# Row normalisation on one core: sharing the last scale between two engines, storing the last tile from ScalarE's queue, and issuing only the first load ahead of the entry barrier

## The chip, the core and the metric

The kernel runs on one core of a Trainium2 chip. The core has several engines that run their own instruction streams and meet through semaphores. Four matter here: VectorE (DVE in the profile), ScalarE (ACT), GpSimd (POOL) and SyncE (SP). TensorE (PE) has no work. Data moves between the device memory (HBM, here called DRAM in the names) and the on-chip memory of 128 partitions by 16 DMA engines, which take transfers from queues. A transfer is issued by an instruction of one engine, and that engine's name is the queue's name in this text.

The metric is the time of one execution on the device in microseconds (us). The median of three runs is 81.77 us, the lowest 81.73 and the highest 81.94.

## The reference

```python
def setup_inputs():
    batch, dim = 1024, 4096
    return {"x": np.random.randn(batch, dim).astype(np.float32), "axis": -1, "eps": np.float32(1e-12)}

def reference(x, axis, eps):
    norm = np.sqrt(np.sum(x ** 2, axis=axis, keepdims=True) + eps)
    return (x / norm).astype(np.float32)
```

Each of 1024 rows of 4096 float32 is divided by the root of its sum of squares. 16.78 MB are read and 16.78 MB written.

## The kernel before, in words

The 1024 rows are cut into two tiles (called tile 0 and tile 1 below). A tile has 128 partitions with R = 4 rows of 4096 values in each, 64 KB in a partition and 8.39 MB in all. Both tiles have their own buffer `xt`, so nothing waits for a buffer to come free. A tile is loaded by one transfer (line 219), scaled in place, and stored by one transfer (line 239). All four transfers are issued by SP.

For each tile (lines 223 to 239) the four rows of a partition are taken as follows. DVE squares and sums row 3 (`square_dve`, line 42) and ACT squares and sums rows 0, 1 and 2 one after the other (`square_act`, line 33). `norm` takes the root on ACT (line 53) and the reciprocal on DVE (line 59). `scale` multiplies a row by its reciprocal norm on DVE (line 64). The rows are scaled in the order 0, 1, 3, 2. For row 2, the last one, tile 0 uses `scale_by_both`: ACT takes the first 7/8 of the columns (3584, line 72) and DVE the remaining 512 (line 78). Tile 1 uses the plain `scale` on DVE. The store of a tile waits for all of its scales.

The program begins with an entry barrier: each engine arrives, GpSimd gathers the arrivals and releases all. `to_front` moves a load out of the body and in front of SP's arrival (its `Drain`) in the entry block. Before the change it is called for both loads, in the order of the tiles, so that SP issues both and then arrives.

At the end there are two barriers (line 271 in the profile). `gpsimd_waits_for_last_store` rewrites the second one: SP waits for everything except the last store before it arrives, and GpSimd, which gathers, waits for the last store's landing before it releases the others. Its argument is the store of tile 1; it finds that store by its semaphore, on whichever queue it is issued.

Of the kernel before, what the change touches and what calls it, by code (L numbers as in the profile page):

```python
# [79 lines left out]
        )  # L80


def to_front(nc, load):

    def move(program):  # L90
        blocks = program.main_func.blocks
        entry = blocks[0].instructions
        if any(i.name == load.name for i in entry):
            return
        body = next(
            b.instructions
            for b in blocks
            if any(i.name == load.name for i in b.instructions)
        )
        at = next(n for n, i in enumerate(body) if i.name == load.name)  # L100
        assert not body[at].sync_info.on_wait
        before = next(
            n
            for n, i in enumerate(entry)
            if i.engine == mybir.EngineType.SP and isinstance(i, mybir.InstDrain)
        )
        entry.insert(before, body.pop(at))

    nc.at_finalize(move)
# [72 lines left out]
@with_exitstack  # L182
def kernel(
    ctx: ExitStack,
    tc: tile.TileContext,
    x: bass.AP,
    axis: bass.AP,
    eps: bass.AP,
    out: bass.AP,
):  # L190
    nc = tc.nc
    P = nc.NUM_PARTITIONS

    assert isinstance(axis, int) and axis in (-1, len(x.shape) - 1)
    eps = float(eps)

    x = x.flatten_outer_dims()
    out_flat = out.flatten_outer_dims()
    N, D = x.shape
    R = 4  # L200
    assert N % (P * R) == 0
    n_tiles = N // (P * R)
    x_t = x.rearrange("(p t r) d -> t p (r d)", t=n_tiles, r=R)
    out_t = out_flat.rearrange("(p t r) d -> t p (r d)", t=n_tiles, r=R)

    io = ctx.enter_context(tc.tile_pool(name="io", bufs=n_tiles))
    scratch_pool = ctx.enter_context(tc.tile_pool(name="scratch", bufs=1))
    stats = ctx.enter_context(tc.tile_pool(name="stats", bufs=n_tiles))

    eps_t = scratch_pool.tile([P, 1], F32)  # L210
    nc.vector.memset(eps_t, eps)  # L211
    sq_act = scratch_pool.tile([P, D], F32)
    sq_dve = scratch_pool.tile([P, D], F32)
    scratch = {"act": sq_act, "dve": sq_dve}

    groups = []
    for i in range(n_tiles):
        g = RowGroups(nc, io, stats, scratch, D, R, eps_t)
        load = nc.sync.dma_start(out=g.flat(), in_=x_t[i])  # L219
        to_front(nc, load.ins)  # L220
        groups.append(g)

    for i, g in enumerate(groups):
        g.square_dve(R - 1)
        g.square_act(0)
        g.norm(0)
        g.scale(0)
        g.square_act(1)
        g.norm(1)
        g.norm(R - 1)  # L230
        g.scale(1)
        g.scale(R - 1)
        g.square_act(2)
        g.norm(2)
        if i < n_tiles - 1:
            g.scale_by_both(2)
        else:
            g.scale(2)
        store = nc.sync.dma_start(out=out_t[i], in_=g.flat())
    gpsimd_waits_for_last_store(nc, store.ins)  # L240


# [33 lines left out]
```

## Time and profile before

The profiled execution took 81.77 us. Its span, from the first to the last instruction of the kernel, is 79.9 us; the remaining 1.87 us lie around the span.

| What | Value |
|---|---|
| Time of the profiled execution | 81.77 us |
| Span | 79.9 us |
| DVE busy | 26.7 us (33%) |
| ACT busy | 29.7 us (37%) |
| DMA queue busy, share of 16 engines | 97.6% |
| Bytes moved, mean rate over the span | 33.55 MB, 420 GB/s |
| Squares on ACT (line 33), each | 3609 ns |
| Square on DVE (line 42), each | 4424 ns |
| Scale of a row on DVE (line 64), each | 2353 ns |
| ACT's part of the shared scale (line 72) | 3282 ns |
| DVE's part of the shared scale (line 78) | 486 ns |

All times in the views count from the span's start. In a line of the timeline the first number is the start, the second the duration, then follow the engine, the line of the kernel, the operation and its operands; a bracket at the end tells the idle time before it and what ended it. A letter q behind an engine's name (SPq) means its sequencer, which issues transfers and waits. In the DMA view a row of numbers divides the window in equal slices; a packet's bytes are counted in the slice in which it begins. "To landing" is the time from a transfer's issue to its last completion.

### The profile page before, as it was taken

The numbers are of one execution on the slowest core, as the hardware profiler recorded it, in microseconds if no ns is written. First come the engines' busy times: TensorE is split into PE (matmuls) and PEld (weight loads), VectorE is DVE, ScalarE is ACT, GpSimd is POOL, SyncE is SP. The second block draws the span as 40 slices with busy tenths as digits, with TensorE's granted clock in tenths as the row PEclk, the third lists the DMA queues.
The fourth block names the chain that finished last, engine by engine and source line by source line (L and its number), as shares of the span: only waits on it lengthen the run. The fifth ranks groups of instructions, "written<-read, shape, count | busy, mean of one in ns | idle before, by whom it ended". The sixth has DMA issues, their size and how long they took to land.

```text
span 79.9 us, 93 instructions
## 1 busy us (share of the span) xinstructions
DVE 26.7 (33%) x21; ACT 29.7 (37%) x23; POOL 0.2 (0%) x4
## 2 busy tenths in 40 slices
DVE  0000000000099599960049995999200000000000
ACT  3200000000099999989349999950000000000000
POOL 1000000000000000000000000000000000000000
DMA  9099996599996699993899991999974999965990
GB/s 492 33 525 525 525 525 295 230 525 525 525 525 262 262 525 525 525 525 164 361 525 525 525 459 66 525 525 525 525 328 197 525 525 525 525 295 230 525 525 0
DMA packets 576, 33.55 MB, mean 420 GB/s; under 512 B 64, under 2 KB 64, under 8 KB 64
## 3 DMA queue, kind: packets, MB, share of 16 engines
q1 hardware_dynamic: 576, 33.55, 97.6%
HBM read 16.78 MB, written 16.78 MB: 420 GB/s over the span
## 4 chain that ended last, share of the span: by engine, by line
DMA 51%; ACT 10%; DVE 9%; SPq 0%; issue 0%
DMA xt<-in_x_dram 51%; ACT sq_act L33 9%; DVE xt L64 9%; ACT rstd L53 1%; SPq L219 0%; DVE rstd L59 0%
## 5 line engine op out<-in xcount | busy, mean ns | idle before, releaser
L33 ACT ACTIVATE sq_act<-xt 128x4096 f32<-128x4096 f32 x6 | 21.7, 3609 | 21.7 <-DMA xt<-in_x_dram 21.7
L42 DVE SCALAR_TENSOR_TENSOR sq_dve<-xt 128x4096 f32<-128x4096 f32 x2 | 8.8, 4424 | 25.7 <-DMA xt<-in_x_dram 25.7
L64 DVE TENSOR_SCALAR xt<-xt,rstd 128x4096 f32<-128x4096 f32 x7 | 16.5, 2353 | 0.2
L72 ACT ACTIVATE xt<-xt,rstd 128x3584 f32<-128x3584 f32 x1 | 3.3, 3282 | 0.2 <-DVE rstd L59 0.2
L53 ACT ACTIVATE rstd<-ssq,eps_t 128x1 f32<-128x1 f32 x8 | 2.1, 289 | 0.1
L59 DVE RECIPROCAL rstd<-rstd 128x1 f32<-128x1 f32 x8 | 1.3, 159 | 2.4 <-ACT rstd L53 2.4
L33 ACT ACT_TABLE_LOAD x1 | 1.3, 1283 | 1.3 <-PEq L257 1.3
L53 ACT ACT_TABLE_LOAD x1 | 1.3, 1283 | 0.0
L33 ACT ACTIVATION_READ_ACCUMULATOR sq_act<-xt 128x1 f32 x6 | 1.1, 186 | 0.0
L211 DVE MEMSET eps_t<- 128x1 f32 x1 | 0.1, 59 | 1.3 <-PEq L257 1.3
L78 DVE TENSOR_SCALAR xt<-xt,rstd 128x512 f32<-128x512 f32 x1 | 0.5, 486 | 0.0
L42 DVE DVE_READ_ACCUMULATOR sq_dve<-xt 128x1 f32 x2 | 0.2, 82 | 0.0
L257 POOL MEMSET const-bfloat16-1.0<- 128x1 bf16 x1 | 0.1, 103 | 0.0
L257 POOL MEMSET const-uint8-127<- 128x1 uint8 x1 | 0.1, 102 | 0.0
L257 POOL MEMSET const-float32-0.0<- 128x1 f32 x1 | 0.1, 100 | 0.2 <-issue 0.2
L257 POOL MEMSET const-float32-1.0<- 128x1 f32 x1 | 0.1, 99 | 0.0
## 6 DMA issues: line engine op xcount, KB each, us to landing
xt<-in_x_dram SPq DMA_DIRECT2D x2, 31.2
out_dram<-xt SPq DMA_DIRECT2D x2, 22.5
```

Source lines behind the costliest of these rows:

```text
L33: self.nc.scalar.activation(out=sq_a, in_=self.x[:, r], func=ACT_F.Square, accum_out=self.ssq[:, r : r + 1],)
L42: self.nc.vector.scalar_tensor_tensor(out=sq_v, in0=self.x[:, r], scalar=1.0, in1=self.x[:, r], op0=ALU.mult, op1=ALU.mult, accum_out=self ...
L53: self.nc.scalar.activation(out=self.rstd[:, r : r + n], in_=self.ssq[:, r : r + n], func=ACT_F.Sqrt, bias=self.eps_t,)
L59: self.nc.vector.reciprocal(out=self.rstd[:, r : r + n], in_=self.rstd[:, r : r + n])
L64: self.nc.vector.tensor_scalar_mul(out=self.x[:, r], in0=self.x[:, r], scalar1=self.rstd[:, r : r + 1])
L72: self.nc.scalar.activation(out=self.x[:, r, :cut], in_=self.x[:, r, :cut], func=ACT_F.Copy, scale=rstd,)
L78: self.nc.vector.tensor_scalar_mul(out=self.x[:, r, cut:], in0=self.x[:, r, cut:], scalar1=rstd)
L211: nc.vector.memset(eps_t, eps)
L257: nc = _bacc.Bacc("TRN2", target_bir_lowering=False, num_devices=1)
```

## The change

Three things change. Only the first tile's load is moved ahead of SP's arrival at the entry barrier; the second tile's load stays in the body and is issued behind the barrier, still by SP. (The function that moves it gets a new name; its body is the same.) The last row of tile 1 is scaled as that of tile 0 is, by ACT and DVE together. And the store of tile 1 is issued by ACT, on ACT's queue, while that of tile 0 stays with SP.

```diff
-def to_front(nc, load):
+def first_load_to_front(nc, load):
...
         load = nc.sync.dma_start(out=g.flat(), in_=x_t[i])
-        to_front(nc, load.ins)
+        if i == 0:
+            first_load_to_front(nc, load.ins)
         groups.append(g)
...
         g.square_act(2)
         g.norm(2)
-        if i < n_tiles - 1:
-            g.scale_by_both(2)
-        else:
-            g.scale(2)
-        store = nc.sync.dma_start(out=out_t[i], in_=g.flat())
+        g.scale_by_both(2)
+        queue = nc.sync if i < n_tiles - 1 else nc.scalar
+        store = queue.dma_start(out=out_t[i], in_=g.flat())
     gpsimd_waits_for_last_store(nc, store.ins)
```

## The prediction, made before the changed kernel was run

> **What bounds the kernel now.** I read the head of the page and its DMA rows first, to see which resource is full.
>
> ```profile
> span 79.9 us, 93 instructions
> DVE 26.7 (33%) x21; ACT 29.7 (37%) x23; POOL 0.2 (0%) x4
> q1 hardware_dynamic: 576, 33.55, 97.6%
> ```
>
> The reader is to see that both computing engines are idle for nearly two thirds of the span while the one DMA queue is busy for 97.6% of it. 576 packets are 512 of data and 64 small ones (the page counts 64 under 512 B), so a data packet is 33.55 MB / 512 = 65.5 KB, and each of the 16 engines moves 32 of them.
>
> Next the four transfers, by their issues and the median time to landing (load 0 alone takes 21.8 us to land and load 1 40.7, since the minimum and maximum for the tile are 21.8 and 40.7; the stores take 21.8 and 23.3).
>
> ```profile
> xt<-in_x_dram SPq DMA_DIRECT2D x2, 31.2
> out_dram<-xt SPq DMA_DIRECT2D x2, 22.5
> 0.00 0.86 SPq L219 DMA_DIRECT2D xt<-in_x_dram  x2
> 38.71 0.35 SPq L239 DMA_DIRECT2D out_dram<-xt  x1
> 56.50 0.34 SPq L239 DMA_DIRECT2D out_dram<-xt  x1
> ```
>
> Landings follow: load 0 at 0.0 + 21.8 = 21.8, load 1 at 0.43 + 40.7 = 41.1, store 0 at 38.7 + 21.8 = 60.5, store 1 at 56.5 + 23.3 = 79.8. The distances are 19.3, 19.4 and 19.3 us, that is, every transfer lands one full transfer time after the one ahead of it, whatever the moment of its issue. The whole span is therefore 21.8 (cold start and first load) + 19.3 + 19.4 + 19.3 = 79.8, and 0.1 for the release at the end. Nothing on the ACT or DVE side is a term of that sum as long as each transfer is queued before the one ahead runs dry.
>
> How early must it be queued? The DMA view over five-microsecond windows answers, since it books a packet where it begins (rates of 1500 to 3100 GB/s in slices of 0.125 us are whole packets counted at once). In order: 0 to 5, 38 to 43 and 58 to 63 us.
>
> ```profile
> GB/s 0 0 0 0 0 0 0 0 3146 2621 0 0 1049 0 524 524 524 0 0 0 0 0 0 0 0 0 0 0 0 0 0 0 1573 3146 524 2097 1049 0 0 0
> ...
> GB/s 1049 1573 2097 0 0 0 0 0 0 0 0 0 0 0 0 0 0 0 2097 2097 1049 2097 1049 0 0 0 0 0 0 0 0 0 0 0 0 0 0 1573 2097 1049
> ...
> GB/s 0 0 0 0 0 0 0 0 0 0 0 0 0 3146 1573 1573 2097 0 0 0 0 0 0 0 0 0 0 0 0 0 0 0 2097 2621 1573 1573 524 0 0 0
> ```
>
> First row: after a cold issue at 0.0 the first packets begin at 1.0 to 2.1 us, and the second round at 4.0 to 4.6. A round in steady state is 19.3 / 8 = 2.4 us, so the cold lag is worth 1.6 to 2.2 us from issue to a packet at full pace. Second row: store 0, issued at 38.71, has its first packets at 40.25 to 40.9, one round after those at 38.0 to 38.4: 1.5 us of lead is enough on this queue, with no hole. Third row: the round that begins at 59.6 to 60.1 is store 1's first. This is the appointment that the changed kernel has to keep.
>
> Last the end of each tile on the engines, and what SP still waits for.
>
> ```profile
> 35.41 3.28 ACT L72 ACTIVATE xt<-xt,rstd 128x3584 f32<-128x3584 f32 x1 [0.23 <-DVE rstd L59]
> 35.41 0.49 DVE L78 TENSOR_SCALAR xt<-xt,rstd 128x512 f32<-128x512 f32 x1
> 53.93 0.15 DVE L59 RECIPROCAL rstd<-rstd 128x1 f32<-128x1 f32 x1
> 54.12 2.35 DVE L64 TENSOR_SCALAR xt<-xt,rstd 128x4096 f32<-128x4096 f32 x1
> SPq L271 <- PEq L271: 19.4, 2, 19.2
> SPq L271 <- DMA out_dram<-xt: 3.2, 1, 3.2
> ```
>
> Store 1 is issued at 56.5, as soon as the 2.35 us scale ends, 3.1 us ahead of 59.6. SP then waits 3.2 us for store 0 and 19.2 us at the exit barrier while store 1 drains.
>
> **The change, part by part.** *First load.* It stays ahead of the barrier at 0.0. Same packets, same 1.0 us: 0.
>
> *Second load.* Its issue (0.43 us) leaves the place ahead of SP's arrival. SP arrives some 0.43 us sooner, at about 0.5 in place of 0.9. GpSimd, the gatherer, has ended its four memsets (the last begins at 0.33 and takes 0.10) and its own drain (0.18 from 0.30) by then, so the barrier falls at about 0.8 in place of 1.2. ACT's first table load and DVE's memset start 0.4 us sooner and then wait for load 0 until 21.8 as before: worth 0. The load itself goes out at about 0.8 and is through by 1.3, some 0.4 later than before. Its first packets are due at 21.0 (1.0 + 8 rounds of 2.4 + the lag), so 19 us of load 0 cover it, and nothing stands between the barrier and it on SP. If that cover were gone it would cost 0.4.
>
> *The shared last scale.* One 2.35 us DVE scale becomes an ACT copy of 3584 columns (3.28 us in tile 0) beside a DVE scale of 512 (0.49). ACT is free: its last work in tile 1 ends at 53.1. The reciprocal that both need still stands behind DVE's scale of row R-1, ends at 54.08, and the next instruction starts at 54.12. ACT then runs 54.12 to 57.40, DVE ends at 54.6. So the sharing makes the last row ready 3.28 - 2.35 = 0.93 us later, not sooner.
>
> *The store on ACT's queue.* ACT issues it behind its own copy, about 57.42 (SP took 0.02 us after the copy in tile 0: 35.41 + 3.28 = 38.69, issue at 38.71). Nothing else of the kernel is queued behind it on ACT but its exit arrival, which moves from about 53 to about 57.8; DVE's arrival (after 54.6) and SP's (after store 0's issue) are sooner. The first of the two exit barriers then closes near 58 in place of 57, and the second one waits for store 0 at 60.5 and then store 1 at 79.8 in any case: 0.
>
> The lead over 59.6 is 59.6 - 57.42 = 2.2 us, against 3.1 before. The trace shows no DMA issued by ACT, so its lag is bounded by two rows: 1.5 us on a running queue (no loss, 0.7 to spare) and 1.6 to 2.2 us on a cold one (57.42 + 2.2 = 59.6: just in time). A loss is open above: if nothing of the cold lag overlaps store 0, it is paid from the landing at 60.5 to 62.7, against 60.1 before, +2.6 us. A gain is excluded here, since the engines have no idle time between 41 and 79 to win back. I take 0, by the cold row, which is the nearest: ACT's queue is as unused at 57.4 as SP's is at 0.0, and the engines are busy with store 0 while it starts.
>
> *Two queues at once.* Store 0's last round starts at 57.2 to 57.7 (59.6 to 60.1 less 2.4), and a cold queue brings its first packets 1.0 us after 57.42, at 58.4. So store 0 has no unstarted packets to interleave with: 0.
>
> The sum: 21.8 + 19.3 + 19.4 + 19.3 + 0.1 = 79.9 us again, and the 1.87 us around the span (81.77 - 79.9). The profiled execution took 81.77, which is also the median shown, so no shift is needed: 81.8 us.
>
> The page "DMA: Bandwidth & Descriptors" of the Trainium skill gives, under "Latency and other measured facts", about 0.6 us to the first byte of a DMA issued from SP or ACT. The first row above has 1.0 to 2.1 us, so the measurement stands; by the page the store would reach the engines at 58.0, with 1.6 us to spare, and the sum would be the same 81.8. The same page, under "Issuing engines are not separate DMA queues", says that DMAs from different engines share the 16 DMA engines and that spreading them saves the issue time alone. That speaks against a gain from ACT's queue: what it could save is SP's 0.34 us issue, which here lies under store 0, so by the rule as by the sum nothing is won.
>
> **The rivals.** (A, slower) ACT's queue starts late. It decides from a lag of 2.2 + 0.25 us after 57.42. For it: the lead shrinks from 3.1 to 2.2, exactly the slow end of the cold lag, and the start of a second queue beside a running one is in no row. Against it: at 38.71 a lead of 1.5 was enough. Price: half as long again as the cold lag, 3.3 us, puts the first packets at 60.7 against 59.6 to 60.1, +0.6 to +1.1, so +0.9: 82.7 us. The whole lag behind store 0's landing would give 84.4.
>
> (B, faster) The second load's issue disturbs the first one's start. The first packets spread over 1.0 to 2.1 us, while the second load's issue ran at 0.43 to 0.86, just ahead of them. If its absence let all engines start a second issue's length sooner, 0.43 us would be won at the front of a gapless chain: 81.35. Against it: the second issue only moves to 0.8 to 1.3, right into the first packets, and eleven of sixteen first packets begin within the first quarter of a microsecond. Moved there it may even disturb more.
>
> (C, slower) A second queue costs something at the launch or the end, in the 1.87 us around the span, which no row breaks up. By one more issue's length, 0.35: 82.1.
>
> (D) The change does not do what it says: ACT's part is not the last to end, or the barrier is held by something else. Either leaves the DMA chain as it is: 81.8, inside the forecast.
>
> **How the numbers follow.** Forecast with D 0.54, A 0.24, C 0.08, B 0.14. Within 0.3% (0.25 us, about what a measurement of this kernel can tell from no change; its three runs span 81.73 to 81.94) is the forecast alone: 0.54. Slower is A and C, 0.32; faster is B, 0.14. The likeliest case alone has 81.6 to 82.0. The range has to reach B's price and A's middle price: 81.4 to 82.7; what is left out is the dearer half of A and the tail of B, under 2 in 10.
>
> **What would show it.** Right: the first load's packets from 1.0 us, the second load's issue at 0.8 to 0.9, landings again near 21.8, 41.1, 60.5 and 79.8, an ACT issue at 57.4, and the DMA view over 58 to 63 with a full round at 59.6 to 60.1 and the next one 2.4 us later. Rival A is a hole in that view, with store 1's landing later by the same amount and SP's exit wait longer. Rival B is a first round closer together and every landing earlier by the same few tenths, from 21.8 on. Rival C leaves the span at 79.9 and lengthens the time alone. The prediction is wrong above all if ACT's first DMA needs more than 2.4 us to bring a packet to an engine.

## The result and the profile after

The changed kernel takes 82.72 us (median of 6 runs, 82.59 to 82.83) where the kernel before took 81.88 (81.73 to 81.98): the ratio is 1.0103, with a 95% interval of 1.0087 to 1.0119. It is slower by 0.84 us. The forecast was no change, and the upper end of its range, 82.7, is 0.02 us short of the median.

The profiled execution took 82.78 us. The first lines of its page, its span and its two DMA queues (packets, megabytes, share of 16 engines), are these:

```profile
span 80.9 us, 94 instructions
...
q1 hardware_dynamic: 432, 25.17, 72.9%
q10 hardware_dynamic: 144, 8.39, 24.9%
```

A second queue, q10, now carries one of the four transfers. The span grew by 1.0 us and the time around it stayed at 1.9 (82.78 - 80.9), so the loss is inside the kernel. The page's list of issues, with the median time to landing, places it:

```profile
xt<-in_x_dram SPq DMA_DIRECT2D x2, 31.2
out_dram<-xt SPq DMA_DIRECT2D x1, 21.8
out_dram<-xt ACTq DMA_DIRECT2D x1, 23.2
```

The timeline has the end of tile 1 on ACT:

```profile
54.28 3.28 ACT L72 ACTIVATE xt<-xt,rstd 128x3584 f32<-128x3584 f32 x1 [1.04 <-DVE rstd L59]
57.59 0.37 ACTq L238 DMA_DIRECT2D out_dram<-xt  x1
```

ACT issues store 1 at 57.59 and it lands 23.2 us later, at 80.8. Store 0 (issued at 38.82) lands at 60.6. Between the two lie 20.1 us, where the kernel before had 19.3. That is 0.8 of the 1.0 us; the other 0.2 is a slightly later landing of both loads in this execution (21.9 and 41.3 in place of 21.8 and 41.1). That part comes and goes: of two runs below with the same two loads, the profiled execution of the one with 2048 columns on ACT has 21.9 and 41.3 too, and that of the one with 4064 has 21.7 and 41.1.

The DMA view, which books a packet where it begins, shows what happened within that transfer. The rows are the windows from 57 to 62 and from 60 to 65 us, in slices of 0.125 us:

```profile
GB/s 0 0 0 2621 2097 2621 524 524 0 0 0 0 0 0 0 0 0 0 0 0 0 0 1049 2622 3670 0 1049 0 0 0 0 0 0 0 0 0 0 0 0 0
...
GB/s 3670 0 1049 0 0 0 0 0 0 0 0 0 0 0 0 0 0 0 0 0 0 0 0 0 0 3670 3670 1049 0 0 0 0 0 0 0 0 0 0 0 0
```

Store 0's last round begins at 57.4 to 57.9, and store 1's first round at 59.8 to 60.4, one packet time of 2.4 us later. So far there is no hole. But store 1's second round does not begin until 63.1 to 63.5. In the view of before, from 58 to 63 us, the round of 59.6 to 60.1 was followed by one at 62.0. The packet records say the same: the sixteen first packets of store 1 last 3.07 to 3.48 us, while every other packet of both stores lasts 2.42. All sixteen engines lose 0.65 to 1.06 us once, in the packet with which they go over from SP's queue to ACT's.

A first packet of that length has one other place in this profile. The first packets of load 0, which start cold, last 2.86 to 3.37 us here. By these rows the hand-over to the other queue costs about what a cold start costs beyond its issue (0.44 to 0.95 us more than 2.42); that the two have one cause is not shown.

### The profile page after: what moved, and what is told of

Read it like the earlier page. It is cut to its first block, busy times and chain, and to the rows that moved or that the text cites. A ratio compares the mean times of both kernels' runs of the same rounds, so it can differ in the third digit from the quotient of the medians.

```text
span 80.9 us, 94 instructions
## 1 busy us (share of the span) xinstructions
DVE 24.9 (31%) x21; ACT 33.0 (41%) x24; POOL 0.2 (0%) x4
## 4 chain that ended last, share of the span: by engine, by line
DMA 50%; ACT 14%; DVE 6%; issue 0%
DMA xt<-in_x_dram 50%; ACT sq_act L33 9%; DVE xt L64 6%; ACT xt L72 4%; ACT rstd L53 1%; DVE rstd L59 0%
## 5 line engine op out<-in xcount | busy, mean ns | idle before, releaser
L33 ACT ACTIVATE sq_act<-xt 128x4096 f32<-128x4096 f32 x6 | 21.7, 3608 | 22.4 <-DMA xt<-in_x_dram 22.4
L64 DVE TENSOR_SCALAR xt<-xt,rstd 128x4096 f32<-128x4096 f32 x6 | 14.1, 2353 | 0.2
L72 ACT ACTIVATE xt<-xt,rstd 128x3584 f32<-128x3584 f32 x2 | 6.6, 3283 | 1.3 <-DVE rstd L59 1.3
L78 DVE TENSOR_SCALAR xt<-xt,rstd 128x512 f32<-128x512 f32 x2 | 1.0, 486 | 0.1
## 6 DMA issues: line engine op xcount, KB each, us to landing
out_dram<-xt SPq DMA_DIRECT2D x1, 21.8
out_dram<-xt ACTq DMA_DIRECT2D x1, 23.2
```

Of the source, the lines that this page charges most:

```text
L33: self.nc.scalar.activation(out=sq_a, in_=self.x[:, r], func=ACT_F.Square, accum_out=self.ssq[:, r : r + 1],)
L64: self.nc.vector.tensor_scalar_mul(out=self.x[:, r], in0=self.x[:, r], scalar1=self.rstd[:, r : r + 1])
L72: self.nc.scalar.activation(out=self.x[:, r, :cut], in_=self.x[:, r, :cut], func=ACT_F.Copy, scale=rstd,)
L78: self.nc.vector.tensor_scalar_mul(out=self.x[:, r, cut:], in0=self.x[:, r, cut:], scalar1=rstd)
```

## The experiments

Ratios are to the kernel before, run on the same chip beside each group of kernels (medians 81.80 to 81.84 us).

**Which part.** Four kernels do the parts one by one. The first is the kernel before with only the store moved to ACT.

```diff
-        store = nc.sync.dma_start(out=out_t[i], in_=g.flat())
+        queue = nc.sync if i < n_tiles - 1 else nc.scalar
+        store = queue.dma_start(out=out_t[i], in_=g.flat())
```

> The kernel before with one part of the change: store 1 is issued by ACT (both loads ahead of the barrier, last scale on DVE alone). The issue should be near 56.5, a lead of about 3.1 us over store 0's end instead of 2.2. New-queue theory (the first packet of each DMA engine on a queue that takes over takes 3.1 to 3.5 us in place of 2.4, whatever the lead): the same 0.65 to 1.05 us longer first round, time +0.7 to +0.9 us, ratio 1.009 to 1.011. Lateness theory (the store was issued too late): with 0.9 us more lead most or all of it goes, time within 0.1 us of before, first round at 2.4 us.

Measured: 81.81 us, ratio 1.0003 (0.9988 to 1.0017). The second is the kernel before with only the last scale shared.

```diff
-        if i < n_tiles - 1:
-            g.scale_by_both(2)
-        else:
-            g.scale(2)
+        g.scale_by_both(2)
```

> The kernel before with one part of the change: the last scale of tile 1 is shared by ACT and DVE, store 1 is issued by SP near 57.4. New-queue theory: no second queue, so nothing: within 0.1 us of before, packets at 2.4 us throughout. Lateness theory: the lead of 2.2 us is as short as in the changed kernel, so the same loss of 0.7 to 0.9 us.

Measured: 81.79 us, ratio 0.9986 (0.9978 to 0.9995). The third moves only the second load.

```diff
-        to_front(nc, load.ins)
+        if i == 0:
+            to_front(nc, load.ins)
```

> The kernel before with one part of the change: only the first load is ahead of the barrier. Both theories put nothing here, within 0.1 us. Third theory (the move of the second load disturbs the start or the loads): +0.1 to +0.2 us, as the changed kernel's load landings of 21.9 and 41.3 stand 0.1 and 0.15 behind those of before.

Measured: 81.81 us, ratio 1.0000 (0.9991 to 1.0009). The fourth is the changed kernel with its last store back on SP.

```diff
-        queue = nc.sync if i < n_tiles - 1 else nc.scalar
-        store = queue.dma_start(out=out_t[i], in_=g.flat())
+        store = nc.sync.dma_start(out=out_t[i], in_=g.flat())
```

> The changed kernel with store 1 given back to SP (shared last scale and the second load behind the barrier stay). New-queue theory: within 0.1 us of before. Lateness theory: still +0.7 to +0.9 us. Third theory: +0.1 to +0.2 us.

Measured: 81.83 us, ratio 1.0000 (0.9990 to 1.0010).

No part loses anything by itself. The second load's place is worth nothing, which disposes of the third theory. A store from SP that is issued as late as in the changed kernel (57.52 in the fourth) loses nothing, so the short lead alone is not the cause. A store from ACT that is issued at 56.47 loses nothing either, so the other queue alone is not the cause, and the new-queue theory falls in the form "whatever the lead". (The second kernel's interval ends just below 1; its 0.14% is less than the 0.3% called no change.) The loss needs both: ACT's queue, and the 0.93 us by which the shared scale delays the issue. In the first run the view from 60 to 65 us has its second round at 62, at full pace:

```profile
GB/s 524 0 0 0 0 0 0 0 0 0 0 0 0 0 0 1049 2621 1573 2097 524 524 0 0 0 0 0 0 0 0 0 0 0 0 0 0 2621 1573 3146 524 524
```

**Lag or boundary.** Two theories can hold for that combination. In one, ACT's issue needs a fixed 3.2 to 3.4 us to reach full pace, and what the lead lacks is lost. In the other, an engine that has already begun the last packet of the old queue when the new queue's work arrives pays a fixed price. The next two kernels move the issue to both sides by changing ACT's share of tile 1's last row; tile 0 keeps its 7/8.

```diff
-    def scale_by_both(self, r):
-        cut = 7 * self.D // 8
+    def scale_by_both(self, r, cut):
...
-        g.scale_by_both(2)
+        g.scale_by_both(2, 7 * D // 8 if i < n_tiles - 1 else 2816)
```

> The changed kernel, with ACT's part of tile 1's last scale cut from 3584 to 2816 columns (DVE takes 1280). ACT's part should take about 0.30 + 0.00083 x 2816 = 2.64 us instead of 3.28, so store 1 is issued by ACT near 56.9 in place of 57.6, a lead of about 2.9 us. Fixed-lag theory (a store issued by ACT beside SP's running queue needs about 3.2 to 3.4 us from issue to full pace: 57.59 to the first round's ends 63.2 to 63.4 less one packet time of 2.42): full pace at 60.2 in place of 59.6 to 60.1, time +0.2 to +0.4 us against before. Boundary theory (an engine that finds the other queue's packet only after it has begun its last one pays a fixed 0.65 to 1.05 us, else nothing): each first packet at 2.4 or at 3.1 to 3.5 us, nothing between, time 0 or +0.85.

Measured: 82.42 us, ratio 1.0074 (1.0058 to 1.0090), that is +0.62; issue at 56.91. As times go, both theories missed here: the lag had +0.2 to +0.4, the boundary 0 or +0.85. The packets decide.

```diff
-        g.scale_by_both(2)
+        g.scale_by_both(2, 7 * D // 8 if i < n_tiles - 1 else 4064)
```

> The changed kernel, with ACT's part of tile 1's last scale raised from 3584 to 4064 columns (DVE takes 32). ACT's part about 3.68 us, issue near 58.0, a lead of about 1.8 us. Fixed-lag theory: full pace at 61.3, first packets of about 3.5 to 3.9 us or a hole of that size, time +1.2 to +1.3 us against before. Boundary theory: the same 3.1 to 3.5 us as in the changed kernel, time +0.85.

Measured: 82.62 us, ratio 1.0096 (1.0079 to 1.0113), that is +0.82; issue at 57.76.

The fixed lag asked for +1.2 to +1.3 in the second of these and got +0.82, the same as the changed kernel: it falls. The first, with 2816 columns, shows the boundary itself. Its rows from 57 to 62 and from 60 to 65 us:

```profile
GB/s 0 1049 2097 2621 1573 524 524 0 0 0 0 0 0 0 0 0 0 0 0 0 0 2097 3146 2097 524 524 0 0 0 0 0 0 0 0 0 0 0 0 0 0
...
GB/s 524 524 0 0 0 0 0 0 0 0 0 0 0 0 0 0 0 0 1049 524 1049 0 0 2097 2097 1573 0 0 0 0 0 0 0 0 0 0 0 1049 524 524
```

In the second row a slice of 524 is one packet. Five engines begin their second packet at 62.2 to 62.6, and eleven at 62.9 to 63.25; in the packet records the five first packets last 2.42 to 2.44 us and the eleven 3.10 to 3.43, with nothing between. The records do not name the engine, but a packet begins 2 ns behind the end of the one ahead of it, so each first packet can be paired with a last one. The engines that had begun store 0's last packet up to 0.49 us behind the issue (56.91) are all long, those that began it 0.64 us or more behind are all at full pace, and between 0.5 and 0.64 there are both. So the boundary runs through the middle of the round here, eleven engines pay and five do not, and the time lies between the two that the theory had allowed. The same rule sorts the other runs: in the changed kernel all last packets begin between 0.16 us before and 0.30 us behind the issue (all sixteen long), in the run with only the store moved between 0.67 and 1.20 us behind it (none long).

The Trainium skill's page "DMA: Bandwidth & Descriptors" ("Latency and other measured facts") gives about 0.6 us from the issue on SP or ACT to the first byte. The boundary at 0.5 to 0.64 us is of that size; that it is the same thing, the time until an engine can know of the new queue's work, is not shown. The shortest time from an issue to a packet on idle engines in these runs is 0.86 us (58.71 to 59.57, in the run with the queues exchanged below). The prediction had put the page's figure aside for the 1.0 us that the first load needs at the start.

**Shift the boundary from the other side.** If the rule holds, the change can be kept whole, queue and sharing included, and cost nothing, provided ACT's share is small enough.

```diff
-        g.scale_by_both(2)
+        g.scale_by_both(2, 7 * D // 8 if i < n_tiles - 1 else 2048)
```

> The changed kernel with ACT's part of tile 1's last scale cut from 3584 to 2048 columns (DVE takes 2048). ACT's part about 2.0 us, store 1 issued by ACT near 56.3, over 0.65 us ahead of the start of store 0's last packets (57.1 to 57.9). Boundary theory: no long first round, time within 0.15 us of before (ratio 0.998 to 1.002).

Measured: 81.78 us, ratio 0.9992 (0.9982 to 1.0002); issue at 56.30, and the second round stands at 61.9 to 62.7 in the window from 60 to 65 us:

```profile
GB/s 524 524 0 0 0 0 0 0 0 0 0 0 0 0 0 1049 2097 524 2097 2097 0 524 0 0 0 0 0 0 0 0 0 0 0 0 0 2621 524 2621 1573 524
```

It is as fast as the kernel before, not faster: no version here beats the DMA chain.

**First use of a queue.** In the next kernel ACT issues a small load into an unused tile at the start, beside the changed kernel's work, so that its queue is no longer new at 57 us.

```diff
+    warm = scratch_pool.tile([P, 16], F32)
+    first = nc.scalar.dma_start(out=warm, in_=x_t[0][:, :16])
+    first_load_to_front(nc, first.ins)
...
+    engine = load.engine
...
-            if i.engine == mybir.EngineType.SP and isinstance(i, mybir.InstDrain)
+            if i.engine == engine and isinstance(i, mybir.InstDrain)
```

> The changed kernel with one more transfer: at the start, ahead of its arrival, ACT issues a load of 128 partitions x 16 columns (8 KB) into an unused tile, so that store 1 is not the first transfer on ACT's queue. If the lag is that of a queue's first use: it is gone, time within 0.2 us of before. If it belongs to each start of a queue that had run empty, or to ACT: still +0.7 to +0.9 us.

Measured: 82.82 us, ratio 1.0124 (1.0103 to 1.0145). All sixteen first packets of store 1 last 3.08 to 3.48 us. The loss does not belong to a queue's first use.

**Does it belong to ACT?** A first attempt to exchange the queues missed its aim.

```diff
-        load = nc.sync.dma_start(out=g.flat(), in_=x_t[i])
+        load = nc.scalar.dma_start(out=g.flat(), in_=x_t[i])
...
-            if i.engine == mybir.EngineType.SP and isinstance(i, mybir.InstDrain)
+            if i.engine == mybir.EngineType.Activation and isinstance(i, mybir.InstDrain)
...
-        queue = nc.sync if i < n_tiles - 1 else nc.scalar
+        queue = nc.scalar if i < n_tiles - 1 else nc.sync
```

> The changed kernel with the two queues exchanged: ACT issues both loads (the first ahead of its own arrival) and store 0, SP issues store 1 near 57.5. If the lag belongs to ACT's issues: SP needs no more than the 1.5 to 2.2 us that the trace of before shows, so the first round of store 1 runs at 2.4 us and the time is within 0.15 us of before. If it belongs to any queue that starts beside a running one: first round again 3.1 to 3.5 us, +0.7 to +0.9 us.

Measured: 100.98 us, ratio 1.2351 (1.2326 to 1.2377). With the loads on ACT the scheduler put DVE's square of tile 1 ahead of tile 0's scales, so store 0 went out at 58.7 and the DMA engines stood empty from about 41 to 59 us. It says nothing on the hand-over it was made for. It shows two other things. Store 0 restarted engines that had stood empty for over 18 us, on ACT's queue, which had moved the loads, and its sixteen first packets lasted 2.44 to 2.46 us. So a queue that has run empty, or an engine that has stood idle, does not make a first packet long by itself. And store 1, issued by SP at 70.6 while store 0 was under way, ran beside it. In the window from 74 to 79 us, with the packets of each queue below,

```profile
GB/s 0 6816 1573 0 0 0 0 0 0 0 0 0 0 0 0 0 0 0 0 0 4194 4194 0 0 0 0 0 0 0 0 0 0 0 0 0 0 0 0 0 2621
...
q10 hardware_dynamic: 21, 1.38, 63.6%
q1 hardware_dynamic: 16, 1.05, 48.4%
```

the round at 74.1 is ACT's, that at 76.6 is SP's and that at 78.9 ACT's again, each 2.42 us behind the last. Going from queue to queue is free here, while both have work waiting. The same page of the Trainium skill, under "Queues, rings and completion order", has each engine take turns between its queues packet by packet; these three rounds agree. The order ahead of them is not explained: SP had issued at 70.6, and the rounds of 71.7 and 74.1 were both still ACT's.

The aimed test keeps the loads on SP. Store 0 goes out from ACT, store 1 from ACT or from SP, and one more ACT copy of 1024 columns into scratch delays store 1 until store 0's last packets have begun.

```diff
-    def scale_by_both(self, r):
+    def scale_by_both(self, r, rest):
...
+        if rest:
+            self.nc.scalar.activation(
+                out=self.scratch["act"][:, :rest],
+                in_=self.x[:, r, :rest],
+                func=ACT_F.Copy,
+                scale=rstd,
+            )
...
-        g.scale_by_both(2)
-        queue = nc.sync if i < n_tiles - 1 else nc.scalar
+        g.scale_by_both(2, rest=0 if i < n_tiles - 1 else 1024)
+        queue = nc.scalar
```

> The changed kernel with both stores on ACT's queue, and with one ACT copy of 1024 columns into scratch (1.05 us) ahead of tile 1's last scale, so that store 1 is issued near 58.7, behind the start of store 0's last packets (58.1 to 58.7). Boundary theory (only a hand-over to another queue pays, and pays once): store 0 is issued near 38.8, behind the start of load 1's last packets, so its first round runs 3.1 to 3.5 us; store 1's first round, on the same queue, runs 2.42 us; time +0.8 to +0.9 us against before. If every late issue by ACT pays: both rounds long, +1.6 to +1.8 us.

Measured: 82.57 us, ratio 1.0088 (1.0075 to 1.0102), that is +0.74. The last line of the edit becomes, in its companion, one with SP for store 1:

```diff
-        queue = nc.scalar
+        queue = nc.scalar if i < n_tiles - 1 else nc.sync
```

> As the run with both stores on ACT's queue (store 0 from ACT, the same ACT copy of 1024 columns into scratch), but store 1 is issued by SP, near 58.7. Boundary theory: the hand-over from SP to ACT at store 0 pays, and that from ACT back to SP at store 1 pays too, first rounds 3.1 to 3.5 us in both: +1.6 to +1.8 us against before. If the loss belongs to ACT's issues alone: store 0 long, store 1 at 2.42 us, +0.8 to +0.9 us.

Measured: 83.43 us, ratio 1.0193 (1.0178 to 1.0209), that is +1.60. The windows from 39 to 44 and from 60 to 65 us, first of the kernel with both stores on ACT:

```profile
GB/s 0 0 0 0 0 0 0 0 0 524 2097 1049 2097 1573 1049 0 0 0 0 0 0 0 0 0 0 0 0 0 0 0 0 0 524 0 0 0 2097 1573 1573 2097
...
GB/s 0 0 0 524 2622 2097 1573 1049 0 0 0 0 0 0 0 0 0 0 0 524 0 0 524 1573 2621 2097 1049 0 0 0 0 0 0 0 0 0 0 0 524 0
```

and then of the one with store 1 on SP:

```profile
GB/s 0 0 0 0 0 0 0 0 0 0 2097 2622 2622 524 524 0 0 0 0 0 0 0 0 0 0 0 0 0 0 0 0 0 0 0 0 0 1573 4719 1049 1049
...
GB/s 0 0 0 524 4719 2097 1049 0 0 0 0 0 0 0 0 0 0 0 0 0 0 0 0 0 0 0 0 0 524 524 1573 4719 1049 0 0 0 0 0 0 0
```

In both kernels store 0, now the first transfer on another queue, begins at 40.2 to 40.9 and has its second round at 43.4 to 44, over 3 us later. Store 1, issued at 58.7 in both, splits them: on the same queue as store 0 its rounds stand at 60.4 to 61 and 62.8 to 63.4, 2.4 us apart, and on the other queue at 60.4 to 60.9 and 63.6 to 64.1, 3.2 us apart. (With both on ACT one engine of sixteen lost only 0.24 us at store 0, 0.19 in a gap and the rest in a first packet of 2.47, and runs 0.5 us ahead of the others. The rule gives no reason for that one; it is the only exception seen.) So the loss belongs neither to ACT nor to lateness: SP pays it too when it takes over from ACT, and ACT does not pay it when it follows itself, at a later issue than the changed kernel's. Each hand-over pays once, 0.74 for one and 1.60 for two.

**Another old queue.** The last kernel leaves store 1 as the changed kernel has it and cuts store 0 into transfers of one row, so that the old queue's packets are short.

```diff
-        store = queue.dma_start(out=out_t[i], in_=g.flat())
+        if i < n_tiles - 1:
+            for r in range(R):
+                cols = slice(r * D, (r + 1) * D)
+                queue.dma_start(out=out_t[i][:, cols], in_=g.x[:, r])
+        else:
+            store = queue.dma_start(out=out_t[i], in_=g.flat())
```

> The changed kernel with store 0 cut into four transfers of one row of every partition each, all on SP, so that its packets are 16 KB and about 0.6 us long instead of 64 KB and 2.42 us. Store 1 is left as in the changed kernel: ACT's queue, issued near 57.6. Boundary theory: store 0's last packets now start near 59.3, over 0.65 us behind the issue, so store 1's first packets are taken over without a loss (if 16 KB packets keep the rate): time within 0.2 us of before. If the loss came from the short lead over store 0's end (2.2 us, as in the changed kernel): still +0.7 to +0.9 us.

Measured: 83.08 us, ratio 1.0154 (1.0139 to 1.0169), that is +1.25 where within 0.2 was expected. The hand-over did what the boundary theory says: ACT issued store 1 at 58.72, 2.3 us ahead of its first packets (61.0), as in the changed kernel, and the windows from 60 to 65 us have its rounds 2.4 us apart, at 61.0 to 61.6 and 63.4 to 64, among the last short packets of SP's rows.

```profile
GB/s 262 262 393 524 786 393 0 786 2622 2622 1573 0 1049 0 0 0 0 0 0 0 0 0 0 0 0 0 0 1573 3670 1049 1049 1049 0 0 0 0 0 0 0 0
```

The time went elsewhere. In the window from 37 to 42 us load 1's last round begins at 37.9 to 38.5, and the row packets behind it only from 41.5, more than 3.4 us later, all on SP's queue:

```profile
GB/s 0 0 0 0 0 0 0 2097 3146 1573 0 1573 0 0 0 0 0 0 0 0 0 0 0 0 0 0 0 0 0 0 0 0 0 0 0 0 262 1049 262 262
```

Why a load's last packets become long (3.4 to 3.9 us) when short store packets follow them in the same queue was not tried further and stays open. For the short packets themselves the rate held (0.61 us for 16 KB).

**What stands.** Shown: the loss sits in one packet per engine at the hand-over from one queue to the other; it depends on whether the new queue's transfer was issued 0.5 to 0.64 us or more before the engine began the old queue's last packet (one engine in one run apart); it does not grow with the lateness (0.64 to 1.07 us in every long packet); it comes on either queue and not on the first use alone. Not shown: why. That the packet behind costs nothing when its work was there before the present packet began, and 0.64 us or more when it came later on another queue, suggests that an engine makes its next packet ready while it moves the present one. That is an argument from these rows; the ACT round of 74.1 in the run with the queues exchanged does not follow from it in so simple a form, since SP's issue at 70.6 was 1.1 us old when the round ahead of it began, and no run looks into the engine.

## Why the prediction was wrong, point by point

- **The sum of four back-to-back transfers** held as a frame: 21.9, then 19.4 twice, and the loss shows up as the one distance that changed, 20.1 in place of 19.3.
- **Second load, priced 0:** right. Its issue moved from 0.43 to 0.78, near the predicted 0.8, and the move alone measures 1.0000.
- **Shared scale, 0.93 us later, priced 0 by itself:** right (0.9986 alone, if anything a trace below 1). The predicted issue of 57.42 was 57.59, the difference being the later load landings of that execution.
- **The store on ACT's queue, "I take 0, by the cold row":** this is the step that failed; it measured +0.84. The bounds were stated (0 to +2.6), and the value was chosen by comparing a lag with the lead over store 0's end, 2.2 us. That lead is not what decides: SP met the same end with the same lead (2.3 us with the shared scale alone) and lost nothing, and neither did ACT at the same lead in the kernel that stores by rows. Counted as the cold row was counted, from the issue to the second round less one packet time, ACT took 3.2 to 3.4 us (57.59 to between 60.8 and 61.0) and not 1.6 to 2.2; but it is no lag, since the price did not follow the issue. What decides is the beginning of store 0's last packet, 57.4 to 57.9, one whole packet time of 2.4 us earlier, and whether the issue stands 0.5 to 0.64 us ahead of that. The row from which "1.5 us of lead is enough" was read is of one queue following itself, and does not carry over to two.
- **"Two queues at once: 0":** the reasoning (no unstarted packets of store 0 are left at 58.4, so nothing interleaves) was true and was read the wrong way round. That nothing is left is the condition of the loss; while packets of both queues wait, changing over costs nothing.
- **Rival A** named the place and, by its middle price of +0.9, nearly the size (82.7 against 82.72), with a chance of 0.24. Its mechanism, a lag longer than the lead, was not the one: the first packets began on time, at 59.8 to 60.4, and lateness beyond the boundary added nothing (1.8 us of lead cost +0.82, 2.3 cost +0.84).
- **Rivals B and C** are out: the load move measured nothing, and the time around the span is unchanged at 1.9 us.
- **The sign by which the text said it would be wrong**, more than 2.4 us from ACT's first issue to a packet, did not occur in that form. A full round did begin at 59.8, 2.3 us behind the issue. The sign that did fail stands earlier in the list, "the next one 2.4 us later": the next round came 3.3 us later, because the time was lost inside the first packets. The text looked in the right window and put its weight on the wrong interval.

## What to carry to other kernels

In a chain of transfers that keeps the DMA engines full, put the next transfer on the queue that is running, or, if it goes on another queue, issue it before the engines begin the running transfer's last packets: here 0.65 us and one packet time (2.4 us for 64 KB) ahead of its end. Moving the last store to the engine that finishes last saved nothing and cost 0.84 us, though each part of the change measures as nothing alone; parts that use up the same slack have to be costed together. A lead that a trace shows to be sufficient is sufficient for the queue on which it was seen.

## What was not expected of the hardware

- The price of a hand-over is 0.65 to 1.06 us per engine in the changed kernel, about what the first packets of load 0 have over the others (2.86 to 3.37 against 2.42 us), although the engine was never idle before it. Engines that had been idle for over 18 us and restarted on the queue that they had used last had first packets only up to 0.04 us longer (2.44 to 2.46).
- Two busy queues were seen to share an engine packet by packet both with packets of one size (64 KB beside 64 KB) and with very unequal ones. In the run with the small load at the start, that transfer of 8 KB needed 21.8 us to land beside load 0:

```profile
warm<-in_x_dram ACTq DMA_DIRECT2D x1, 8.0 KB, 21.8
```

  Each of its 64-byte packets waited for one of 64 KB, eight times over.
- A load's last packets on SP's queue ran 3.4 to 3.9 us when 16 KB store packets followed them, unexplained.
